# A transformer chain on one core: the last square of each norm goes straight into the summing products, and modulation columns move in their stage

## The chip, the cores and the metric

The kernel runs on 1 core of one Trainium2 chip. The metric is the device time of one execution in microseconds (us). TensorE does the matmuls, VectorE and ScalarE the element-wise work, GpSimd a few small operations, and SyncE (SP) issues the transfers from memory.

## What is computed

Two blocks run one after the other on 256 tokens of 1024 features, all in float32. Block one has two layers, each with a mixer (causal attention with forget gates, a short convolution and a pooling branch, merged by gates) and a feed-forward part. Block two has two layers as well, the first with a latent-attention mixer and the second with a dilated-attention mixer, each followed by a feed-forward part of 4096 features. Block two is modulated: six vectors per layer are computed from one vector `c` and scale, shift or gate the stream.

```python
cond = jax.nn.silu(c)
for i in range(2):
    mod = (cond @ ada_w[i] + ada_b[i]).reshape(B, 6, D)
    h = rms_norm(x, norm_mix[i]) * (1 + scale1) + shift1
    y = mla_mixer(h, ...) if i == 0 else dilated_mixer(h, ...)
    x = x + gate1 * y
    h = rms_norm(x, norm_mlp[i]) * (1 + scale2) + shift2
    x = x + gate2 * (jnp.square(jax.nn.relu(h @ mlp_w1[i])) @ mlp_w2[i])
```

with `rms_norm(x, g) = x * rsqrt(mean(x * x) + 1e-6) * g`, the mean taken over the 1024 features of a token.

## The kernel before

The stream `x` is held as eight tiles of 128 features by 256 tokens (features on the partitions). Weights come from memory in chunks of up to 1 MB into four raw buffers (`raw`). Each chunk is split into a high and a low part by `split_piece` (ScalarE casts `whi`, L319; VectorE subtracts `wlo`, L320), and every product is done as three matmuls of such parts in `mm3` (L368 to L374). `use` runs the transfers up to four chunks and the splits up to two chunks ahead.

**The norm.** The class `Norm` collects the sum of squares while the eight tiles of `x` are produced. For each tile m, ScalarE squares it (L441) and, from m = 1 on, GpSimd or VectorE adds it to the running sum (L446). `part1` sums the 128 partitions on TensorE by products with a matrix of ones (L452, one per half of the tokens; the hardware runs each as two instructions), VectorE scales and adds epsilon (L409), and GpSimd raises to the power -1/2 (L410). `part2` spreads the result over the partitions by products with the identity (L460). There are eight norms in all. Six of them are closed inside a projection that already runs on unnormalised inputs. The two at the start of the layers of block two are closed by `ada_h`, which has to have the result before it can form the inputs `h` (L1166 to L1170); `keep_warm` puts filler products (L1152) on TensorE around its steps.

**The modulation.** `ada_units(i)` is a generator: each step computes one of the 48 columns of `mod` of a layer, as a product and sum over 1024 elements on VectorE (L629). Every second step first issues the transfer of the next pair of columns (1 MB, L624) into one of the four raw buffers that the weights use too. Callers draw steps at fixed places of the loops. Steps of layer 1 carry a priority lowered by 3000.

**The stage around the change.** `mlp(i, h, tasks)` first runs 16 pairs of output tiles of the first matrix (loop over j = 0, 2, ..., 30; `fin` closes a tile), then eight output tiles of the second one (loop over m), each of which ends in `upd(m, a)`: the new `x[m]` (L1185), its square and its addition. With i = 0 it draws modulation steps. After it come `ada_finish(1, 0)`, the late `ada_h`, and the dilated attention of layer 1, where 24 further steps are drawn; `drain(ada1)` then runs whatever is left, just before the attention's output projection is finished and `mlp(1, h)` begins.

**What sets the order.** A planner orders each engine's instructions ahead of time by priority and by its own estimate of when things are ready; every engine then runs its queue strictly in that order. In the dilated attention stage and in the norm before it, TensorE's order is that of the program. `prio(m)` raises the updates of tiles 5 to 7.

Of the kernel before, what the change touches and what calls it, by code (L numbers as in the profile page):

```python
# [246 lines left out]
def tile_net(ctx, tc, wts, ada, xin, cols_in, table_in, fb_in, c_in, pos_in, inv_in, mask_in, freq_in, out):  # L247
# [22 lines left out]
    def bt(shape=(128, 512), dt=F32):  # L270
        return mk(big, list(shape), dt, "b")
# [4 lines left out]
    def t1(shape=(128, 256), dt=F32):  # L276
        return mk(t1p, list(shape), dt, "t1")
# [4 lines left out]
    def sm(n=1):  # L282
        return mk(smp, [128, n], F32, "sm")

    def acc():
        return mk(accp, [128, 512], F32, "acc")

    def att():
        return mk(attp, [128, 512], F32, "att")

    def cst(shape, dt, name):
        return const.tile(list(shape), dt, tag=name, name=name)

    V, S, G, PE = nc.vector, nc.scalar, nc.gpsimd, nc.tensor
# [67 lines left out]
    def mm3(o_ap, w, sl, x, start, stop, wmov=False, ns=324):  # L362


        whi, wlo = w[0][:, sl], w[1][:, sl]
        xhi, xlo = x
        if wmov:
            PE.matmul(out=o_ap, lhsT=xhi, rhs=whi, start=start, stop=False)  # L368
            PE.matmul(out=o_ap, lhsT=xhi, rhs=wlo, start=False, stop=False)  # L369
            PE.matmul(out=o_ap, lhsT=xlo, rhs=whi, start=False, stop=stop)  # L370
        else:
            PE.matmul(out=o_ap, lhsT=whi, rhs=xhi, start=start, stop=False)  # L372
            PE.matmul(out=o_ap, lhsT=whi, rhs=xlo, start=False, stop=False)  # L373
            PE.matmul(out=o_ap, lhsT=wlo, rhs=xhi, start=False, stop=stop)  # L374
        tick(ns)
# [9 lines left out]
    ones = cst([128, 128], F32, "ones")  # L385
# [20 lines left out]
    def rsqrt_small(r, ss, n, scale):  # L406

        v = sm(n)
        V.tensor_scalar(out=v[:, :n], in0=ss, scalar1=scale, scalar2=EPS, op0=ALU.mult, op1=ALU.add)  # L409
        G.tensor_tensor(out=r, in0=v[:, :n], in1=mhalf[:, :n], op=ALU.pow)  # L410
# [18 lines left out]
    class Norm:  # L429
# [9 lines left out]
        def add_(self, m, xt):  # L439
            q = t1()  # L440
            S.activation(out=q, in_=xt, func=AF.Square)  # L441
            if m == 0:
                self.s = q
            else:
                s = t1()
                (G if m < 6 and self.slow else V).tensor_tensor(out=s, in0=self.s, in1=q, op=ALU.add)  # L446
                self.s = s

        def part1(self):
            ps = att()  # L450
            for tt in range(2):
                PE.matmul(out=ps[:, 2 * tt:2 * tt + 2], lhsT=self.s[:, tt * 128:tt * 128 + 128],  # L452
                          rhs=ones[:, :2], start=True, stop=True)
            self.R = sm(2)
            rsqrt_small(self.R[:, :2], ps[:, 0:4:2], 2, 1.0 / D)

# [26 lines left out]
    def split_plain(dst, src):  # L483
        S.copy(out=dst[:, 0, :], in_=src)
        V.tensor_tensor(out=dst[:, 1, :], in0=src, in1=dst[:, 0, :].bitcast(F32), op=ALU.subtract)

    def parts(tl, sl=slice(None)):
        return tl[:, 0, sl], tl[:, 1, sl]
# [325 lines left out]
    def f1(bl, i0, xs, o_ap):  # L814
        for k, xt in enumerate(xs):
            w, sl = bl.at(i0 + k)
            mm3(o_ap, w, sl, xt, k == 0, k == len(xs) - 1)

    for l in range(2):
# [41 lines left out]
        for which in range(2):  # L861
# [8 lines left out]
            for tt in range(2):  # L870
                ps = a2[tt]
# [150 lines left out]
        bl, i = blk_state["bl"], blk_state["i"]  # L1022
# [49 lines left out]
        def upd(m, a):  # L1072
            with prio(m):
                upd_(m, a)
# [99 lines left out]
    def gated_update(i, s, nx, nrm, final=False, hs=None):  # L1174


        def upd(m, a):
            with prio(m):
                upd_(m, a)

        def upd_(m, a):
            xt = mk(xpool, [128, 256], F32, "x")
            gc = mod[:, 48 * i + 24 * s + 16 + m:48 * i + 24 * s + 17 + m]
            assert modc[0] >= 48 * i + 24 * s + 17 + m
            V.scalar_tensor_tensor(out=xt, in0=a[:, :256], scalar=gc, in1=x[m], op0=ALU.mult, op1=ALU.add)  # L1185
            nx.append(xt)
            if final:
                nc.sync.dma_start(out=out[m * 128:m * 128 + 128, :], in_=xt)
            else:
                if hs is not None:  # L1190
                    ht = mk(hpool, [128, 2, 264], F32R, "h")
                    o_ = 16 * i + 8 + m
                    split_scaled(ht[:, :, :256], xt, Gc[:, o_:o_ + 1])
                    sc = mod[:, 48 * i + 24 + m:48 * i + 25 + m]
                    S.copy(out=ht[:, 0, 256:258], in_=sc.to_broadcast([128, 2]))
                    V.tensor_tensor(out=ht[:, 1, 256:258], in0=sc.to_broadcast([128, 2]), in1=ht[:, 0, 256:258].bitcast(F32), op=ALU.subtract)
                    hs.append(ht)
                nrm.add(m, xt)
        return upd

    def mlp(i, h, tasks=None):
        bl = Blocks()
        hp_ = [parts(t, slice(0, 258)) for t in h]
        mid = []

        def fin(a):
            sh = sm(1)
            S.copy(out=sh, in_=a[:, 256:257])
            r = t1()
            V.tensor_tensor(out=r, in0=a[:, :256], in1=RB, op=ALU.mult)  # L1210
            S.activation(out=r, in_=r, func=AF.Relu, bias=sh)
            S.activation(out=r, in_=r, func=AF.Square)
            y = bt([128, 2, 256], F32R)
            split_plain(y, r)
            mid.append(y)

        held = []
        for j in range(0, 32, 2):
            a2 = [acc(), acc()]
            for k in range(8):  # L1220
                for e in range(2):
                    w, sl = bl.at((j + e) * 8 + k)
                    mm3(a2[e][:, :258], w, sl, hp_[k], k == 0, k == 7, ns=327)
                if j == 0 and k == 7:
                    nrm.part1()
                if j == 2 and k == 1:
                    nrm.part2()
                    RB, _ = nrm.rows(False)
                    fin(held[0])
                    fin(held[1])  # L1230
            if tasks is not None and j >= 4:
                next(tasks, None)
            if j == 0:
                held = a2
            else:
                for e in range(2):
                    fin(a2[e])
        mp = [parts(t) for t in mid]
        final = i == 1
        nrm2 = Norm()  # L1240
        nx = []
        upd = gated_update(i, 1, nx, nrm2, final)
        for m in range(8):
            a = acc()
            f1(bl, 256 + m * 32, mp, a[:, :256])
            upd(m, a)
            if tasks is not None:
                for _ in range(2):
                    next(tasks, None)
        bl.end(512)  # L1250
        return nx, nrm2
# [209 lines left out]
    out_proj8(bl, [parts(t) for t in oT], gated_update(0, 0, nx, nrm, hs=h), ahead_done[0])  # L1461
    x = nx
    x, nrm = mlp(0, h, chain(ada0, ada1))
    ada_finish(1, 0)

# [160 lines left out]
    out_proj8(bl, [parts(t) for t in oT], gated_update(1, 0, nx, nrm, hs=h), acs)  # L1626
    x = nx
    mlp(1, h)


# [33 lines left out]
```

## Time and profile before

| | |
|---|---|
| median of 3 runs | 1572.71 us (1570.24 to 1573.25) |
| the profiled execution | 1576.66 us, its span 1574.9 us |
| TensorE busy | 1550.7 us, 98% |
| VectorE busy | 1177.0 us, 75% |
| ScalarE busy | 899.6 us, 57% |
| GpSimd busy | 152.3 us, 10% |
| mean granted TensorE clock | 0.995 |
| moved from and to memory | 320.77 MB, mean 204 GB/s |

The span reaches from the first to the last instruction of one profiled execution; the execution's own time has a little more around it. Busy shares are means over all stages. Matmuls are pipelined, so the start-to-start distance of two matmuls is shorter than the duration that the trace gives to one.

### The profile page before, as it was taken

To read this page: it belongs to the slowest core of one execution; us is meant where nothing else is said; L and a number is where in the kernel's file an instruction comes from. 1 tells how busy PE (TensorE), PEld (TensorE's weight loads), DVE (VectorE), ACT (ScalarE), POOL (GpSimd) and SP (SyncE) were. 2 spreads that over 40 slices of the span, in tenths; PEclk is the share of its full clock that TensorE was granted. 3 is DMA by queue.
4 is the path that set the end of the run, shared out by engine and by line. 5 is a ranking of instruction groups with operands and counts; after the bars stand their busy time and mean duration, and the time that the engine had idled before them with its cause. 6 is when DMAs were issued, how large, how long until landed. Compare 5 with 4: busy or idle time off the path is not lost.

```text
span 1574.9 us, 31147 instructions
## 1 busy us (share of the span) xinstructions
PE 1550.7 (98%) x12314; PEld 1508.7 (96%) x12314; DVE 1177.0 (75%) x2430; ACT 899.6 (57%) x1854; POOL 152.3 (10%) x209
## 2 busy tenths in 40 slices
PE   9999999999999999999999999999999999999999
PEld 8899999999899999999987899999999999999999
DVE  7877877789787777778778688766777777686642
ACT  7575554443657454443268677533676766677632
POOL 2100100000210010000021100010223222110000
PEclk9999999999999999999999999999999999999999
DMA  8446566655655666665544278775666767655551
GB/s 308 174 173 218 208 241 216 235 183 170 209 193 190 232 227 226 214 240 179 170 133 138 81 244 284 272 270 201 218 213 213 221 199 241 195 203 186 191 198 41
DMA packets 83921, 320.77 MB, mean 204 GB/s; under 512 B 31984, under 2 KB 34800, under 8 KB 58944
## 3 DMA queue, kind: packets, MB, share of 16 engines
q1 hardware_dynamic: 83184, 317.30, 58.6%
q8 instruction: 97, 1.59, 0.4%
q0 software_dynamic: 448, 1.38, 0.3%
q14 instruction: 48, 0.39, 0.1%
q10 hardware_dynamic: 144, 0.11, 0.0%
HBM read 311.42 MB, written 7.34 MB: 202 GB/s over the span
## 4 chain that ended last, share of the span: by engine, by line
PE 91%; DVE 5%; issue 1%; ACT 1%; POOL 1%; DMA 1%; SPq 0%; ACTq 0%; DVEq 0%; POOLq 0%
PE acc L372 21%; PE acc L374 21%; PE acc L373 21%; PE acc L368 6%; PE acc L370 6%; PE acc L369 6%; DVE wlo L320 2%; PE att L767 1%; PE att L1546 1%; POOL sm L410 1%; PE att L1548 1%; PE att L1560 1%; PE att L680 1%; PE acc L713 1%; PE att L1577 1%
## 5 line engine op out<-in xcount | busy, mean ns | idle before, releaser
L320 DVE TENSOR_TENSOR wlo<-raw,whi 128x1024 fp32r<-128x1024 f32 (+2 forms) x508 | 582.3, 1165 | 150.7 <-ACT whi L319 149.8
L319 ACT CAST whi<-raw 128x1024 fp32r<-128x1024 f32 (+2 forms) x508 | 495.2, 1000 | 306.0 <-PE acc L373 183.3
L372 PE MATMUL acc<-b,whi 128*128 128x256 f32 x1744 | 496.4, 285 | 3.2 <-DVE sm L409 1.6
L373 PE MATMUL acc<-b,whi 128*128 128x256 f32 x1744 | 490.2, 281 | 0.0
L374 PE MATMUL acc<-b,wlo 128*128 128x256 f32 x1744 | 489.2, 281 | 0.0
L372 PE MATMUL acc<-h,whi 128*128 128x256 f32 (+1 forms) x1216 | 343.2, 282 | 0.0
L374 PE MATMUL acc<-h,wlo 128*128 128x256 f32 (+1 forms) x1216 | 342.4, 282 | 0.0
L373 PE MATMUL acc<-h,whi 128*128 128x256 f32 (+1 forms) x1216 | 341.5, 281 | 0.0
L372 PEld LDWEIGHTS acc<-b,whi 128*128 128x128 f32 x1744 | 328.3, 188 | 7.3 <-issue 4.0
L373 PEld LDWEIGHTS acc<-b,whi 128*128 128x128 f32 x1744 | 328.5, 188 | 1.2 <-issue 0.8
L374 PEld LDWEIGHTS acc<-b,wlo 128*128 128x128 f32 x1744 | 328.6, 188 | 0.1
L372 PEld LDWEIGHTS acc<-h,whi 128*128 128x128 f32 x1216 | 229.9, 189 | 0.0
L374 PEld LDWEIGHTS acc<-h,wlo 128*128 128x128 f32 x1216 | 229.2, 188 | 0.0
L373 PEld LDWEIGHTS acc<-h,whi 128*128 128x128 f32 x1216 | 229.1, 188 | 0.0
L368 PE MATMUL acc<-whi,h 128*128 128x384 f32 (+4 forms) x544 | 193.3, 356 | 1.9 <-ACT whi L319 1.9
L369 PE MATMUL acc<-wlo,h 128*128 128x384 f32 (+4 forms) x544 | 184.1, 339 | 0.4 <-DVE wlo L320 0.4
L370 PE MATMUL acc<-whi,h 128*128 128x384 f32 (+4 forms) x544 | 182.8, 338 | 0.0
L410 POOL TENSOR_TENSOR sm<-sm,mhalf 128x4 f32<-128x4 f32 (+3 forms) x72 | 93.0, 1292 | 508.8 <-DVE sm L409 468.9
L629 DVE CUSTOM_DVE_ANT_0 t<-raw,cond,cols 128x1024 bf16<-128x1024 f32 x96 | 121.7, 1278 | 11.3 <-DMA raw<-in_ada_dram 5.7
L368 PEld LDWEIGHTS acc<-whi,h 128*128 128x128 f32 x544 | 104.1, 192 | 6.1 <-ACT whi L319 2.1
L369 PEld LDWEIGHTS acc<-wlo,h 128*128 128x128 f32 x544 | 104.1, 191 | 3.4 <-DVE wlo L320 0.6
L370 PEld LDWEIGHTS acc<-whi,h 128*128 128x128 f32 x544 | 103.2, 190 | 2.8
(255 smaller groups left out, 1638.6 us busy)
## 6 DMA issues: line engine op xcount, KB each, us to landing
raw<-in_wts_dram SPq DMA_DIRECT2D x194, 1024.0 KB, 4.8
raw<-in_ada_dram SPq DMA_DIRECT2D x48, 1024.0 KB, 4.9
raw<-in_wts_dram SPq DMA_DIRECT2D x50, 768.0 KB, 4.5
scr<-b SPq DMA_DIRECT2D x48, 128.0 KB, 3.8
b<-scr SPq DMA_DIRECT2D x64, 96.0 KB, 5.3
raw<-in_wts_dram SPq DMA_DIRECT2D x6, 576.0 KB, 4.0
raw<-in_wts_dram SPq DMA_DIRECT2D x6, 512.0 KB, 3.5
raw<-in_wts_dram SPq DMA_DIRECT2D x3, 528.0 KB, 4.1
```

Source lines behind the costliest of these rows:

```text
L319: S.copy(out=hi[:, a:b], in_=r[:, a:b])
L320: V.tensor_tensor(out=lo[:, a:b], in0=r[:, a:b], in1=hi[:, a:b].bitcast(F32), op=ALU.subtract)
L368: PE.matmul(out=o_ap, lhsT=xhi, rhs=whi, start=start, stop=False)
L369: PE.matmul(out=o_ap, lhsT=xhi, rhs=wlo, start=False, stop=False)
L370: PE.matmul(out=o_ap, lhsT=xlo, rhs=whi, start=False, stop=stop)
L372: PE.matmul(out=o_ap, lhsT=whi, rhs=xhi, start=start, stop=False)
L373: PE.matmul(out=o_ap, lhsT=whi, rhs=xlo, start=False, stop=False)
L374: PE.matmul(out=o_ap, lhsT=wlo, rhs=xhi, start=False, stop=stop)
L410: G.tensor_tensor(out=r, in0=v[:, :n], in1=mhalf[:, :n], op=ALU.pow)
L629: V.tensor_tensor_reduce(out=junk, in0=w[:, e * 1024:e * 1024 + 1024], in1=cond, scale=1.0, scalar=col("ada_b", n), op0=ALU.mult, op1=ALU. ...
L680: PE.matmul(out=ps[:, 256 * i:256 * i + 256], lhsT=qk[:, 0, 128 * i:128 * i + 128], rhs=qk[:, 1, :], start=True, stop=True)
L713: PE.matmul(out=o_, lhsT=vcol(h0 + e, 0), rhs=pt[:, 0:256], start=True, stop=False)
```

## The change

In `Norm` the square of tile 7 is no longer added to the running sum. `part1` multiplies both the sum of the first seven squares and the last square with the matrix of ones and accumulates the two in the same place: four products instead of two. In `mlp` the modulation steps begin at j = 2 instead of j = 4, and none are drawn after output tiles 6 and 7. The stage so draws 15 + 12 = 27 steps instead of 14 + 16 = 30; three more are left for `drain(ada1)`, five instead of two.

```diff
             if m == 0:
                 self.s = q
+            elif m == 7:
+                self.last = q
             else:
...
-            for tt in range(2):
-                PE.matmul(out=ps[:, 2 * tt:2 * tt + 2], lhsT=self.s[:, tt * 128:tt * 128 + 128],
-                          rhs=ones[:, :2], start=True, stop=True)
+            for i, s in enumerate((self.s, self.last)):
+                for tt in range(2):
+                    PE.matmul(out=ps[:, 2 * tt:2 * tt + 2], lhsT=s[:, tt * 128:tt * 128 + 128],
+                              rhs=ones[:, :2], start=i == 0 and tt == 0, stop=i == 1 and tt == 1)
...
-            if tasks is not None and j >= 4:
+            if tasks is not None and j >= 2:
                 next(tasks, None)
...
-            if tasks is not None:
+            if tasks is not None and m < 6:
                 for _ in range(2):
                     next(tasks, None)
```

## Rows read from the trace of the kernel before

**Rows 1.** The page's busy table: engine, busy us, share of the span, instructions.
```profile
PE 1550.7 (98%) x12314; PEld 1508.7 (96%) x12314; DVE 1177.0 (75%) x2430; ACT 899.6 (57%) x1854; POOL 152.3 (10%) x209
```
**Rows 2.** TensorE's timeline, early norm: start, duration, instruction, [idle before <-releaser].
```profile
782.98 1.05 PE L1152 MATMUL att<-ones 128*128 128x128 f32 x8
786.38 0.58 PE L452 MATMUL att<-ones,t 128*128 128x2 f32 x4 [2.34 <-DVE t L446]
```
**Rows 3.** TensorE's timeline, late norm.
```profile
1087.35 1.73 PE L1152 MATMUL att<-ones 128*128 128x128 f32 x14
1091.24 0.61 PE L452 MATMUL att<-ones,t 128*128 128x2 f32 x4 [2.17 <-DVE t L446]
...
1093.18 1.23 PE L460 MATMUL att<-ident,sm 128*128 128x128 f32 x4 [0.78 <-POOL sm L410]
1094.19 2.77 PE L1152 MATMUL att<-ones 128*128 128x128 f32 x12
1096.62 0.67 PE L368 MATMUL acc<-whi,h 128*128 128x384 f32 x1
```
**Rows 4.** TensorE's timeline, the norm inside the projection at 910 us.
```profile
910.18 0.50 PE L452 MATMUL att<-ones,t 128*128 128x2 f32 x4
910.54 0.36 PE L372 MATMUL acc<-h,whi 128*128 128x258 f32 x1
```
**Rows 5.** VectorE's timeline (DVE), late norm.
```profile
1087.09 1.28 DVE L629 CUSTOM_DVE_ANT_0 t<-raw,cond,cols 128x1024 bf16<-128x1024 f32 x1 [2.60 <-DMA raw<-in_ada_dram]
...
1089.50 0.48 DVE L1185 SCALAR_TENSOR_TENSOR x<-acc,mod,x 128x256 f32<-128x256 f32 x1
```
**Rows 6.** ScalarE's timeline (ACT), late norm.
```profile
1087.47 0.83 ACT L319 CAST whi<-raw 128x768 fp32r<-128x768 f32 x1 [4.10 <-issue]
1090.08 0.42 ACT L441 ACTIVATE t<-x 128x256 f32<-128x256 f32 x1 [1.77 <-DVE x L1185]
```
**Rows 7.** The chain that ended last, before the late norm: start, duration, what.
```profile
1081.70 5.36 DMA raw<-in_ada_dram
```
**Rows 8.** ScalarE's timeline, early norm.
```profile
784.58 0.41 ACT L441 ACTIVATE t<-x 128x256 f32<-128x256 f32 x1
```
**Rows 9.** VectorE's timeline, early norm.
```profile
784.09 1.80 DVE L320 TENSOR_TENSOR wlo<-raw,whi 128x768 fp32r<-128x768 f32 x2
...
786.99 0.16 DVE L409 TENSOR_SCALAR sm<-att 128x2 f32<-128x2 f32 x1 [0.76 <-PE att L452]
```
**Rows 10.** One line's instructions, L446 and L452: count, duration min/median/max in ns, starts.
```profile
L446 DVE TENSOR_TENSOR t<-t,t x31: 407/419/426, 6.4 to 1392.0; 128x256 f32<-128x256 f32 x31
...
L452 PE MATMUL att<-ones,t x32: 167/251/330, 16.9 to 1394.5; 128*128 128x2 f32 x32
```
**Rows 11.** Stretches: us, busy of five engines, granted clock, DMA share, GB/s.
```profile
404.00:406.00 2.00, 1.34 (x11) 1.12 (x10) 1.54 (x3) 0.03 (x1) 1.50 (x1) 1.00 0.91 348
1094.00:1096.00 2.00, 2.00 (x11) 2.00 (x11) 1.56 (x4) 1.04 (x3) 0.00 (x0) 0.50 0.85 353
```
**Rows 12.** TensorE's timeline, the norms closed at 201 and 403 us.
```profile
205.03 0.71 PE L460 MATMUL att<-ident,sm 128*128 128x128 f32 x4 [0.55 <-POOL sm L410]
...
406.17 0.71 PE L460 MATMUL att<-ident,sm 128*128 128x128 f32 x4 [0.83 <-POOL sm L410]
```
**Rows 13.** The chain that ended last, behind the late norm.
```profile
1097.28 0.32 PE acc L369
...
1099.78 0.17 PE acc L369
```
**Rows 14.** VectorE's timeline, end of the dilated attention.
```profile
1375.61 0.42 DVE L485 TENSOR_TENSOR b<-att,b 128x256 fp32r<-128x256 f32 x1 [0.42 <-ACT b L484]
```
**Rows 15.** Stretches, the output projection after that attention.
```profile
1376.00:1395.00 19.00, 19.00 (x163) 18.92 (x162) 18.39 (x34) 14.90 (x32) 4.85 (x5) 1.00 0.59 194
```
**Rows 16.** GpSimd's timeline (POOL), the power in two norms.
```profile
404.50 1.62 POOL L410 TENSOR_TENSOR sm<-sm,mhalf 128x2 f32<-128x2 f32 x1 [80.62 <-DVE sm L409]
...
1092.42 0.71 POOL L410 TENSOR_TENSOR sm<-sm,mhalf 128x2 f32<-128x2 f32 x1 [15.10 <-PE att L1152]
```

## The prediction, made before the changed kernel ran

> **What bounds the kernel now.** I read the page's busy table first: TensorE is busy in 98% of the span [rows 1]. The kernel is a stream of matmuls; an edit on another engine counts only where TensorE stands still for it, while every product added to the stream counts in full. Next the list of TensorE's waits: the two longest on this code are at the summing products of two norms, L452, with 2.34 us at 786 us and 2.17 us at 1091 us, both for VectorE's last addition L446 [rows 2, 3]. These are the two norms that `ada_h` closes before any input of the next projection can be formed; I call them the early and the late one. The other six are closed inside running projections: at 910 us the products stand between projection matmuls with no gap [rows 4].
>
> The late norm is to be read engine by engine. The matmuls of output tile 7 end at about 1087.5, the filler products of `keep_warm` run from 1087.35 for 1.73 us, and then TensorE idles until 1091.24 [rows 3]. VectorE could have formed `x[7]` at once, but in its queue two modulation columns (L629) stand ahead: it first waits 2.60 us for their transfer, starts them at 1087.09, and `x[7]` starts only at 1089.50 [rows 5]. The square follows on ScalarE at 1090.08 [rows 6], then on VectorE a split piece and the addition. The chain that ended last goes through this very transfer [rows 7]. At the early norm no column stands in front: the square starts at 784.58 [rows 8], and VectorE is in two split pieces for 1.80 us from 784.09 before it can add [rows 9].
>
> **Columns no longer beside tiles 6 and 7.** Four columns leave the output loop and one (j = 2) joins the pair loop: 27 instead of 30 in the stage, 67 instead of 70 before the attention stage, where `ada_finish(1, 0)` needs 64. Without columns `x[7]` can start when its matmuls end, at 1087.5 instead of 1089.50: 2.0 us earlier. Its square comes behind a cast that holds ScalarE for 0.83 us from 1087.47 [rows 6], so it ends near 1088.7 instead of 1090.5.
>
> **Last square straight into the products.** One addition of 0.42 us per norm leaves VectorE [rows 10]. That is worth something only in the two exposed norms: there TensorE can sum the first seven squares ahead and waits for the last square alone.
> Late norm: TensorE comes out of the filler at 1089.08 (1087.35 + 1.73). The products of the old sum, four instructions, take 0.36 us by the norm at 910 us [rows 4], with the start after a gap some 0.4; so the last products start at 1089.5, when the square is long done, instead of 1091.24: **1.7 us**. Bounds: 0.8 if the power on GpSimd is slowed (below), 2.0 if all of the shift of `x[7]` comes through.
> Early norm: the old sum's products run in the idle time after the filler, which ends at 784.03 (782.98 + 1.05) [rows 2]; the last ones start behind the square at 785.05 (784.58 + 0.41 and a hand-over) instead of 786.38, 1.3 us earlier. But the scaling L409, now at 786.99, sits behind the split pieces that end at 785.89 [rows 9]. That leaves **1.1 us**. Bounds: 0.2, if the scheduler puts one more piece of 0.9 us (half of the two) in front of L409, and 1.3.
>
> **The clock.** After the late norm the granted clock is 0.50, the level of 1.2 GHz, in the window from 1094 to 1096 [rows 11]; before it TensorE had idled for 2.17 and 0.78 us [rows 3]. At 404 us it idled for 0.83 us alone and kept 1.00 [rows 11, 12]. After the change the late norm has some 0.9 us left, the wait for the power. What the low level costs: the first eight projection matmuls follow at 0.32 instead of 0.17 us [rows 13], 1.2 us; and the last twelve filler products take 2.43 us (1094.19 to 1096.62) where 14 took 1.73 [rows 3], 0.9 us, of which 0.6 counts, since the first `h` tile is then what is late next. I credit 1.0 of these 1.8, because the last `h` tiles, paced by VectorE, come due; bounds 0 and 1.8. For the early norm, whose idle time falls from 2.8 to about 1.3 us, I credit 0.3 of at most 0.9 us, half of the late norm's.
>
> **More products.** Each norm gets four more instructions at L452; now 32 serve eight norms [rows 10]. Four take 0.36 us up to the next matmul [rows 4], and that is paid in full at the norms of 586, 910 and 1394 us: 1.1 us. The first norm, at 17 us, runs on the lower clock; I take 0.4. At 201 and 403 us TensorE waits for the power afterwards anyway, 0.55 and 0.83 us [rows 12], behind a scaling that stands after a split piece: nothing is paid while that wait lasts, 0.36 us each without it. Together **1.5 us** lost; bounds 1.1 and 2.3.
>
> **Where the columns go.** The j = 2 column costs VectorE some 1.3 us near 910 us, hidden as long as the weight split runs a chunk ahead of TensorE; I take nothing, 1.3 us if that cover is gone. The 24 columns of the attention stage keep their places, their transfers move by one. At its end five columns are drained instead of two, and two transfers instead of one stand in front of the weights' on SP's queue. The pair drained now leaves VectorE a wait of 0.42 us before it splits the last attention output [rows 14]; behind that it is busy for 18.39 of 19 us [rows 15]. The three more columns (3.8 us) are gate columns of the last output loop and can wait until that stretch is over. I take nothing; bounds 0 and 4 us.
>
> **Sum.** -1.7 - 1.1 - 1.0 - 0.3 + 1.5 = -2.6 us. The profiled execution took 1576.66 us (span 1574.9 and 1.8 around it), 0.25% above the median 1572.71 of the runs shown. From its own time that gives 1574.1, from the median 1570.1.
>
> **Rivals.**
> *The gap shrinks, but little comes of it.* The power takes 0.71 us where VectorE is quiet and 1.62 us with a split piece right behind the scaling [rows 16]. As the late norm moves forward against the splits, a piece can fall just there: 0.9 us lost. If the clock falls all the same, 1.3 more. The edit may also miss its mark: columns are low-priority work that the scheduler fills in, and one whose data has landed may still stand in front of `x[7]`; then the late norm gives about the 0.7 us of addition and split piece. Each leaves between -0.3 and -1.7: about 1571.8.
> The Trainium skill, "SBUF — State Buffer", section "Who interferes with whom", says that a VectorE instruction with two SBUF inputs and a GpSimd instruction that reads SBUF shut each other out for their whole length, whoever starts first. The two durations of the power agree with it; by that rule the sum would be -1.7 with a piece there in one norm.
> *The clock stays up throughout.* 1.8 and 0.9 instead of 1.0 and 0.3: -4.0, or 1568.7. For it speaks the little idle time left; against it that the filler is thin work itself.
> *Slower: the drained columns.* If two of them are queued ahead of the updates of the attention's output projection, and their transfer is late by what the pair at 1087 waited, 2.60 us [rows 5], VectorE loses that and 2.5 us for the two, in a stretch where it has 0.6 us to spare [rows 15]. TensorE would lose some 4.5 us: net +1.9, 1574.6. The sign turns once that loss exceeds 2.6 us. Against it: low priority, and the one pair of now fits.
>
> **How the numbers follow.** Forecast 0.50 (own range 1568.5 to 1571.5), little comes of it 0.25, clock stays up 0.13, drained columns 0.12. A difference under 0.2%, 3.1 us, can hardly be told from none. The forecast's -2.6 crosses that line only with more of the clock's credit: a third of it and nearly all of the clock case make faster 0.29; slower takes most of the last case, 0.11; same is the rest, 0.60. The range, 1567.5 to 1575.0, reaches from the clock case with its bounds to the slow case.
>
> **What would show it.** Right: no L629 between tile 5's and the late norm's `x[7]`; `x[7]` within 0.1 us of the end of its matmuls; eight L452 instructions per norm, and the 31 additions on VectorE [rows 10] down to 23; the stall at the late L452 gone and the early one under 1 us; a shorter low stretch of the clock. Wrong: a column or a late transfer still in front of `x[7]`, new stalls between 1375 and 1400 us, or a power of 1.6 us in either exposed norm.

## The result, and the profile after

The changed kernel takes 1591.18 us (median of 4 runs, 1589.73 to 1592.19), the kernel before beside it 1572.98: a ratio of 1.0112, interval 1.0100 to 1.0123. It is **18 us slower**; the forecast was 1570.1, the range 1567.5 to 1575.0. The profiled executions show less of it. They took 1589.73 and 1576.66 us (spans of 1587.4 and 1574.9), the first 1.45 us below its median, the one of before 3.68 above: 13.07 + 1.45 + 3.68 = 18.20.

The page's busy table of the changed kernel, to be read against [rows 1]:

```profile
PE 1556.9 (98%) x12346; PEld 1513.4 (95%) x12346; DVE 1174.9 (74%) x2422; ACT 899.1 (57%) x1854; POOL 154.3 (10%) x209
```

The 32 further products and the 8 additions fewer on VectorE are there; TensorE is busy for 6.2 us more, the span is 12.5 longer. (Behind L452 the lines of the new kernel are numbered three higher; in the kernels with the old norm they are those of before.)

**The norms came out as forecast**, in the two traces. TensorE's timeline of the late norm, against [rows 3]:

```profile
1087.63 1.73 PE L1155 MATMUL att<-ones 128*128 128x128 f32 x14
1089.19 0.95 PE L455 MATMUL att<-ones,t 128*128 128x2 f32 x8
...
1091.82 0.71 PE L463 MATMUL att<-ident,sm 128*128 128x128 f32 x4 [1.13 <-POOL sm L410]
1092.37 1.50 PE L1155 MATMUL att<-ones 128*128 128x128 f32 x12
1093.65 0.44 PE L368 MATMUL acc<-whi,h 128*128 128x384 f32 x1
```

and VectorE's, against [rows 5]:

```profile
1087.83 0.48 DVE L1188 SCALAR_TENSOR_TENSOR x<-acc,mod,x 128x256 f32<-128x256 f32 x1 [3.06 <-PE acc L374]
...
1090.18 0.16 DVE L409 TENSOR_SCALAR sm<-att 128x2 f32<-128x2 f32 x1 [0.61 <-PE att L455]
1090.26 0.95 DVE L320 TENSOR_TENSOR wlo<-raw,whi 128x768 fp32r<-128x768 f32 x1
```

`x[7]` waits for its matmuls and nothing else, the eight products run without a stall, and from the filler's start to the first projection matmul it is 6.02 us (1087.63 to 1093.65) where it was 9.27. At the early norm the last products wait 0.67 us for the square instead of 2.34 for the addition, and TensorE is at the next step 1.1 us sooner:

```profile
785.20 0.61 PE L455 MATMUL att<-ones,t 128*128 128x2 f32 x4 [0.67 <-ACT t L441]
```

Behind the late norm the granted clock is now 1.00 throughout (1092 to 1102 us), where it was 0.50 from 1094 to 1098. Behind the early norm it still falls to 0.50 (788 to 790 us; before, 790 to 792).

**Where the time went.** GpSimd's power L410 runs 76 times in each kernel and makes good marks. The table gives its start, minus that in the profiled execution of before, at eight of them, and the same difference of the spans. (The first column holds what differs up to 587 us, most of it by chance: it is subtracted where stretches are compared. With the new norm 0.36 to 0.37 us of it are no chance: they arise between the marks at 439 and 587 us, in every kernel that has it and in no other, around the norm closed at 586 us.)

| kernel | 587.46 | 787.24 | 910.96 | 1109.00 | 1127.22 | 1137.91 | 1360.04 | 1395.24 | span |
|---|---|---|---|---|---|---|---|---|---|
| changed | +0.08 | -1.01 | -0.52 | -5.63 | -4.60 | +1.72 | +2.02 | +11.65 | +12.5 |
| changed, second profile | +0.46 | -0.65 | -0.15 | -5.26 | -4.23 | +2.10 | +3.13 | +12.33 | +13.3 |
| before, second profile | -0.49 | -0.50 | -0.49 | -3.37 | -3.36 | -3.49 | -3.38 | -3.39 | -3.4 |
| norm alone | +0.79 | -0.30 | +0.20 | -3.05 | -3.10 | -2.84 | -3.04 | -2.76 | -1.8 |
| 28 steps | +1.88 | +0.79 | +1.26 | -2.01 | -2.06 | -1.70 | -1.99 | +0.09 | +2.5 |
| pairs recut | +1.41 | +0.31 | +0.78 | -2.47 | -2.52 | -2.54 | -2.46 | -0.38 | +0.9 |
| pair closed at the end | +0.93 | -0.17 | +0.37 | -4.74 | -3.70 | +2.63 | +3.38 | +9.04 | +11.5 |
| bias loads on GpSimd | -0.83 | -1.93 | -1.50 | -6.62 | -5.46 | -4.34 | -4.60 | -1.01 | +1.7 |
| columns alone | -1.46 | -1.47 | -1.87 | -7.87 | -6.82 | -0.50 | +0.54 | +5.96 | +6.9 |
| odd alone | +0.74 | +0.73 | +0.76 | -3.97 | -2.93 | +3.40 | +4.36 | +9.49 | +10.4 |
| 30 steps | +0.70 | -0.39 | -1.26 | -4.53 | -4.57 | -4.61 | -4.51 | -4.22 | -3.3 |

By 1109 us the changed kernel is 5.7 us ahead, of which it gives 1.0 back by 1127. Then it loses 6.3 us in one place, between 1127 and 1138 us, and 9.6 us in another, between 1360 and 1395 us. The first loss and most of the second lie in the dilated attention of layer 1, a stage that the diff doesn't touch. What the diff does touch there is the parity of its columns: two steps share one transfer and one raw buffer, and an odd number, 27, was drawn before the stage.

*The first loss.* SyncE's queue in the changed kernel (a row is a run of transfers of one kind; b is the bias of the attention scores, read back from `scr` in eight loads for each group of heads):

```profile
1106.66 10.61 SPq L310 DMA_DIRECT2D raw<-in_wts_dram  x4
1117.37 5.80 SPq L1539 DMA_DIRECT2D b<-scr  x8
1123.26 0.56 SPq L627 DMA_DIRECT2D raw<-in_ada_dram  x1
1125.84 8.55 SPq L310 DMA_DIRECT2D raw<-in_wts_dram  x3
```

and in the kernel before:

```profile
1120.80 4.48 SPq L310 DMA_DIRECT2D raw<-in_wts_dram  x3
1125.37 8.26 SPq L1536 DMA_DIRECT2D b<-scr  x8
1133.73 0.56 SPq L310 DMA_DIRECT2D raw<-in_wts_dram  x1
1134.38 0.38 SPq L624 DMA_DIRECT2D raw<-in_ada_dram  x1
```

Before, three weight chunks were under way ahead of the bias; now the columns' transfer takes a buffer first and the weights start at 1125.84. VectorE, then TensorE, show what that does:

```profile
1132.21 1.83 DVE L320 TENSOR_TENSOR wlo<-raw,whi 128x768 fp32r<-128x768 f32 x2 [4.66 <-ACT whi L319]
1133.96 1.28 DVE L632 CUSTOM_DVE_ANT_0 t<-raw,cond,cols 128x1024 bf16<-128x1024 f32 x1
...
1135.16 0.55 DVE L1553 CUSTOM_DVE_ANT_0 t<-att,b 128x384 f32<-128x384 f32 x1
```

```profile
1137.85 0.52 PE L1563 MATMUL att<-ident,t 128*128 128x128 f32 x3 [4.00 <-DVE sm L1555]
```

The split of the late weights, and a column behind it, stand in VectorE's queue ahead of the scores (L1553); TensorE, in program order, stands still for 4.00 us. Behind this wait the granted clock falls too (columns as in [rows 11]):

```profile
1140.00:1142.00 2.00, 2.00 (x8) 1.81 (x8) 0.97 (x4) 0.00 (x0) 1.39 (x2) 0.50 0.00 0
```

It is 1.00 again from 1144 us. The next products of L1563 start 5.97 us after these (1143.82); in the kernel before the distance is 4.36 us (1137.50 to 1141.86). TensorE is busy all the time between them, so the clock costs another 1.6 us.

*The second loss.* Here the roles are turned. The pair issued at 1347.46 is split: its second column is drawn only by `drain` (L632 at 1379.12), and it holds one of the four buffers until then. Each weight transfer now waits for a buffer, and the bias loads of the last group wait behind it. The chain that ended last:

```profile
1359.35 5.04 DMA b<-scr
...
1364.41 1.39 DVE wlo L320 x2
1365.81 0.02 issue
1365.83 0.33 SPq L310
1366.16 0.05 issue
1366.21 7.35 DMA b<-scr
```

The split pieces end at 1365.80 and free a buffer, the weight transfer is issued at 1365.83, and only then the last five bias loads, from 1366.21. In the kernel before seven of the eight are issued in one run:

```profile
1355.91 5.20 SPq L1536 DMA_DIRECT2D b<-scr  x7
```

In the changed kernel VectorE and TensorE wait for them:

```profile
1373.72 0.56 DVE L1553 CUSTOM_DVE_ANT_0 t<-att,b 128x384 f32<-128x384 f32 x1 [5.00 <-DMA b<-scr]
```

```profile
1376.07 0.52 PE L1563 MATMUL att<-ident,t 128*128 128x128 f32 x3 [3.00 <-DVE t L657]
1378.21 0.87 PE L1563 MATMUL att<-ident,t 128*128 128x128 f32 x3 [0.92 <-DVE t L657]
```

Then the clock goes, as the stretches show (columns as in [rows 11]):

```profile
1370.00:1378.00 8.00, 4.29 (x34) 3.86 (x33) 2.45 (x11) 2.00 (x8) 0.00 (x0) 0.98 0.33 65
1378.00:1386.00 8.00, 6.32 (x45) 5.28 (x46) 2.90 (x9) 2.32 (x9) 0.00 (x0) 0.50 0.40 132
```

TensorE was busy for 4.29 of 8 us, and for the 8 us after that the granted clock is 0.50, the level of 1.2 GHz.

*A wait behind both.* It is not the pair's. At the last norm the drained columns stand on both sides of the scaling L409 in VectorE's queue, the power comes late, and TensorE waits for it:

```profile
1405.45 1.28 DVE L632 CUSTOM_DVE_ANT_0 t<-raw,cond,cols 128x1024 bf16<-128x1024 f32 x1
...
1406.65 0.15 DVE L409 TENSOR_SCALAR sm<-att 128x2 f32<-128x2 f32 x1
1406.73 1.27 DVE L632 CUSTOM_DVE_ANT_0 t<-raw,cond,cols 128x1024 bf16<-128x1024 f32 x1
```

```profile
1408.62 0.71 PE L463 MATMUL att<-ident,sm 128*128 128x128 f32 x4 [1.63 <-POOL sm L410]
```

In the kernel before TensorE doesn't wait there; with the norm alone it waits 0.50 us, with 28 steps 2.20 and with the pairs recut 2.25. Both have no pair across a border, so it is the number of drained columns that counts here, and it makes up most of the 2.1 us that they lose between the last two marks.

### The profile page after: what moved, and what is told of

Same layout as the page of the kernel before. It is cut to its first block, busy times and chain, and to the rows that moved or that the text cites. A ratio compares the mean times of both kernels' runs of the same rounds, so it can differ in the third digit from the quotient of the medians.

```text
span 1587.4 us, 31205 instructions
## 1 busy us (share of the span) xinstructions
PE 1556.9 (98%) x12346; PEld 1513.4 (95%) x12346; DVE 1174.9 (74%) x2422; ACT 899.1 (57%) x1854; POOL 154.3 (10%) x209
## 4 chain that ended last, share of the span: by engine, by line
PE 89%; DVE 5%; issue 2%; ACT 2%; POOL 1%; DMA 1%; POOLq 0%; SPq 0%; DVEq 0%; ACTq 0%
PE acc L372 21%; PE acc L374 21%; PE acc L373 21%; PE acc L368 6%; PE acc L370 6%; PE acc L369 6%; DVE wlo L320 2%; POOL sm L410 1%; PE att L770 1%; DMA b<-scr 1%; PE att L1549 1%; PE att L1563 1%; PE att L1551 1%; PE att L683 1%; PE acc L716 1%
## 5 line engine op out<-in xcount | busy, mean ns | idle before, releaser
L410 POOL TENSOR_TENSOR sm<-sm,mhalf 128x4 f32<-128x4 f32 (+3 forms) x72 | 95.2, 1323 | 511.8 <-DVE sm L409 478.3
L632 DVE CUSTOM_DVE_ANT_0 t<-raw,cond,cols 128x1024 bf16<-128x1024 f32 x96 | 122.1, 1279 | 7.2 <-PE att L699 3.4
```

Source lines behind the costliest of these rows:

```text
L632: V.tensor_tensor_reduce(out=junk, in0=w[:, e * 1024:e * 1024 + 1024], in1=cond, scale=1.0, scalar=col("ada_b", n), op0=ALU.mult, op1=ALU. ...
```

## The experiments

My theory: it is the pair that lies across the border between two stages. It shifts the transfers of the whole attention stage by one step and leaves a buffer occupied at the end, and SyncE's queue, in which weights and bias loads stand in one line, turns both into stalls. Two rivals: the three more columns drained beside the last norm; and the new norm, which moves the planner's order everywhere behind it.

**The norm alone** (columns as in the kernel before).

```diff
-            if tasks is not None and j >= 2:
+            if tasks is not None and j >= 4:
...
-            if tasks is not None and m < 6:
+            if tasks is not None:
```

> The norm part alone, columns as before. Theory (an odd number of modulation steps in the stage splits a pair of columns, so that one raw buffer stays occupied and the weight and bias transfers behind it on SP's queue come late): the norm part is innocent, 1570 to 1573 us (early norm -1.0, late norm about -0.7, more products +1.0), no stall between 1120 and 1140 or 1365 and 1385 us. Rival 1 (more columns and transfers to drain at the end of the attention): the same. Rival 2 (the norm edit moves the planner's order and so the stalls): 1585 us or more.

1574.19 us, ratio 1.0005 (0.9993 to 1.0016), a little above the expected range. The norm loses nothing that the times show, and gains nothing either: a question for later.

**The columns alone** (the kernel before, with the columns of the changed one).

> The column part alone, norm as before: 27 steps, five columns drained. Theory and rival 1: both stalls are there, 1589 to 1593 us. Rival 2: about 1571 us.

1584.99 us, ratio 1.0071 (1.0054 to 1.0088). Both losses are there: TensorE waits 4.0 us for VectorE in the first, and the last power starts 5.4 us later, counted from the one at 1360 us. But that is 5.4 and not 9.6 us, and the time is 4 us short of the expected range: the old norm has a smaller second loss (see the last experiment).

**One more step**: 28 drawn, four drained, still two transfers in the drain.

```diff
-                for _ in range(2):
+                for _ in range(3 if m == 5 else 2):
```

> The changed kernel with a third step after output tile 5: 28 steps, an even number, four columns and two transfers drained. Theory: no pair is split at the start or the end of the attention stage, both stalls go, the gain at the norms stays: 1567 to 1571 us. Rival 1: four instead of five columns and still two transfers, 1584 to 1591 us.

1576.81 us, ratio 1.0018 (1.0008 to 1.0028). One step more takes away 14 of the 18 us; the time is far from the rival's range, but 6 us above that of the theory. The first loss is gone (-2.06, then -1.70 in the table). Between the last two marks 2.1 us are left, most of them the delay of the last power by the drained columns.

**Odd alone**: the kernel before with one step fewer, at the front (29 drawn, three drained in one transfer, columns beside all tiles, old norm).

```diff
-            if tasks is not None and j >= 4:
+            if tasks is not None and j >= 6:
```

> The kernel before with steps from j = 6 on instead of j = 4: 29 steps, an odd number; columns still beside tiles 6 and 7, three columns and one transfer drained. Theory: the split pair alone brings both stalls, 1582 to 1590 us. Rival 1: one column more and no transfer more than before, 1573 to 1577 us.

1585.23 us, ratio 1.0072 (1.0056 to 1.0088). A single step taken from the kernel before costs 11 us, with one more column drained and no more transfer for it: what costs is that the number of steps is odd.

**The pair closed at the end**: the changed kernel, one more step in the last attention group.

```diff
-            if n_ in (2, 10, 19):
+            if n_ in (2, 10, 19) or (hp == 7 and n_ == 22):
```

> The changed kernel with one more column step, drawn in the last attention group (27 + 25 steps, 4 columns drained), so that the second column of the last pair leaves its buffer before the attention ends. The first loss of the changed kernel (6.3 us between the GpSimd powers at 1127 and 1138 us) is not touched. Theory (a transfer brings two columns; an odd number of steps in the MLP stage leaves a pair half used at the stage's end and moves every later transfer by one step): the first loss stays at 6 to 6.5 us, the second (9.6 us between the powers at 1360 and 1395 us) shrinks to 1 to 6 us, because the buffer comes free but the bias loads still stand behind weight transfers on SP: 1582 to 1588 us beside 1574 of the kernel before. Rival (what costs is the columns drained beside the last norm): one column fewer there, two transfers still: 1590 us, with both losses as they were.

1587.58 us, ratio 1.0086 (1.0067 to 1.0106). The first loss is untouched (6.3 us), the second 5.7 instead of 9.6: both as the theory has it.

**The bias loads on GpSimd's queue**, otherwise the changed kernel.

```diff
-                nc.sync.dma_start(out=b_[64 * e:64 * e + 64], in_=src.rearrange("(s q) k -> q s k", q=64))
+                nc.gpsimd.dma_start(out=b_[64 * e:64 * e + 64], in_=src.rearrange("(s q) k -> q s k", q=64))
```

> The changed kernel with the 64 bias loads of the attention groups issued by GpSimd instead of SP. Theory (the stalls come because bias loads and weight transfers stand in one line on SP, behind a transfer that waits for one of the four buffers): the waits for the bias loads near 1374 us go, the second loss falls from 9.6 to 2 to 5 us, and the first, where weights stand behind the waiting transfer, at least shrinks: 1578 to 1586 us. Rival (SP's order is not what counts, but that a buffer is held): both losses stay, 1589 to 1593 us. If GpSimd's own instructions wait behind these loads, its powers and split pieces come late all through the attention, and the time is above 1593 us.

1578.77 us, ratio 1.0034 (1.0022 to 1.0045). The split pair is still there and holds its buffer, but 12 us are gone: the first loss shrinks from 6.3 to 1.1 us, the second from 9.6 to 3.6. TensorE has no wait left near 1130 us, and its longest at the end is 2.26 us at the last norm, as with the pairs recut. So the held buffer alone does little in this kernel; what made it dear is that one queue carries both.

**The pairs recut**: 27 steps and five drained columns as in the changed kernel, but the column at each border comes in a transfer of its own.

```diff
-        for n0 in range(0, 48, 2):
+        cut = [*range(0, 48, 2), 48] if i == 0 else [*range(0, 20, 2), *range(19, 48, 2), 48]
+        for n0, n1 in zip(cut, cut[1:]):
```

> The changed kernel, its 27 steps and its 5 drained columns unchanged, but the pairs cut anew: the 19th column of the second half (the last one of the MLP stage) comes in a transfer of its own, and so does the last, so that no pair lies across a border of stages; one more transfer in all. Theory (it is the pair across the border, not the number of steps or of drained columns): SP's order in the attention stage is that of the kernel before, both losses go, and what the three drained transfers cost at the last norm stays: 1575 to 1579 us. Rival (five drained columns cost it): 1588 to 1592 us.

1577.20 us, ratio 1.0021 (1.0010 to 1.0032). The steps, and the columns beside the last norm, are those of the changed kernel; 14 us are gone. One stretch of this kernel and the same of the changed one, where TensorE idles for 4.00 of 16 us:

```profile
1124.00:1140.00 16.00, 16.00 (x101) 15.69 (x100) 11.23 (x30) 9.32 (x24) 4.98 (x8) 1.00 0.84 244
```

```profile
1124.00:1140.00 16.00, 12.00 (x71) 11.52 (x70) 9.50 (x22) 7.17 (x18) 1.28 (x4) 0.96 0.64 220
```

**Thirty steps**, none beside the last two tiles, two drained.

```diff
-                for _ in range(2):
+                for _ in range(3 if m < 3 else 2):
```

> The changed kernel with three column steps instead of two beside the first three output tiles: 15 + 15 = 30 steps in the MLP stage as before, 2 columns drained in one transfer as before, none beside the last two tiles. Theory: the transfers of the attention stage stand where they stood before, both losses go entirely, and what is left is the gain at the two norms that the traces of the changed kernel showed (1.0 at the first, 1 to 2 more by the last, up to 5.6 by the first attention group at 1109 us, of which the kernel of before's columns with the new norm already has 3): 1570 to 1573 us beside 1574 of the kernel before. Rival (something else of the columns' new places costs, so that only the old places are good): 1576 us or more.

1574.74 us, ratio 1.0004 (0.9992 to 1.0015). Neither loss is left in the trace, and its span is 3.3 us under that of before. Yet the median is the same and misses the expected range. The same columns with the old norm, run next, complete the four combinations.

> The kernel before with the columns of the 30-step placement (from output pair 2 on, three beside the first three output tiles, two beside the next three, none beside the last two) and its old norm. With it the four combinations of old and new norm and old and good columns are complete. By the sum of the prediction: without the new norm the early gap stays as it is (its 2.3 us idle time), the late one loses the columns in front of the last tile (1.5 to 2.5 us) if those cost anything in most executions: 1571 to 1573 us beside 1574; if they cost only in the profiled execution of before: 1574, no change.

1574.82 us, ratio 1.0004 (0.9993 to 1.0014): same, as expected if the columns in front of `x[7]` cost only in the execution that I had read. And with 32 steps and no column left to drain (`range(2 if m == 5 else 3)`):

> The changed kernel with three steps beside each of the first five output tiles and two beside the sixth: 32 steps in the MLP stage, 24 in the attention, no column left to drain beside the last norm, none beside the last two tiles. Theory (a pair across a border and columns drained at the end are what costs): both losses of the changed kernel are gone and the end gains what the two drained columns of the kernel before cost beside its last norm, 0.5 to 2 us: 1570 to 1573.5 us. Rival (the denser columns in the MLP stage keep VectorE and SP's line from the split pieces there): 1575 us or more.

1574.62 us, ratio 1.0002 (0.9991 to 1.0012): same, a little above the range expected by the theory and just under the rival's 1575.

**The kernel before once more**, for a second profile: it asks where the norm's gain of the first traces has gone.

> The kernel before once more, unchanged, for a second profile of it. In the traces so far everything that the new norm saves adds up to about 2.6 us between the GpSimd powers at 587 us and the end (first norm 1.1 saved, the norm at 911 us 0.5 lost, last norm 1.4 saved by its power and 1.8 more by the first attention group, the end 0.9 lost), yet the kernel with the new norm alone has the same median as before. Theory A (the profiled execution of before was a slow one at its last norm: the column transfer in front of the last residual tile was issued at 1081.70 us there and at 1080.0 to 1080.2 in the two experiments that keep it, which save their 1.7 by that alone): the second profile shows the transfer near 1080, an idle time of 0.6 us instead of 2.17 before the summing products, and the power about 1.5 us earlier. Theory B (the late transfer belongs to the kernel): 2.2 us again, and the medians hide a real gain in the spread of the runs' starts.

Theory A. The median is 1573.93 us (ratio 1.0005, 0.9993 to 1.0018), but at the late norm of the second profile SyncE issues the transfer early, and TensorE hardly waits:

```profile
1078.73 0.38 SPq L624 DMA_DIRECT2D raw<-in_ada_dram  x1
```

```profile
1086.85 1.73 PE L1152 MATMUL att<-ones 128*128 128x128 f32 x14
1089.19 0.61 PE L452 MATMUL att<-ones,t 128*128 128x2 f32 x4 [0.61 <-DVE t L446]
...
1094.21 0.62 PE L368 MATMUL acc<-whi,h 128*128 128x384 f32 x1
```

0.61 us instead of 2.17, and 7.36 us from the filler to the projection instead of 9.27. From the mark at 587 to that at 1109 this execution is 2.9 us shorter than the one that I had read.

**VectorE made to wait for the power**: with new norm and no column drained, a small copy of the power's result on VectorE right behind it.

```diff
             rsqrt_small(self.R[:, :2], ps[:, 0:4:2], 2, 1.0 / D)
+            V.tensor_copy(out=sm(2)[:, :2], in_=self.R[:, :2])
```

> The kernel with no column drained and the new norm (32 steps in the MLP stage), and one small copy of the norm's two columns on VectorE behind the power, so that VectorE's next instruction waits for GpSimd's power instead of running beside it. In all traces with the new norm a split piece stands directly behind the scaling, and the power takes 1.72 us at 911 us, 1.28 to 1.29 at 1092 us and 1.62 to 1.72 at the last norm, where it takes 0.71 in the kernel before. In VectorE's order the copy stands directly behind the scaling at all norms but two; at those two (near 586 and 1092 us) one split piece is still between them. Theory (VectorE's work beside the power slows it): 0.71 us at 404, 911 and at the last norm, still about 1.3 at 1092, TensorE's waits for the power at 911 and at the last norm (0.50 each) gone: 1.0 us shorter there, up to 1 us more at 404 us: 1572.5 to 1574 us beside 1574.6 of the same kernel without the copy. Rival (the new norm's power is slow for its own reason, or the late split pieces cost what the power saves): durations or time as without the copy, 1574 to 1576 us.

The power in the norm at 910 us, with the norm alone and with the copy, and the stretch around it in the same order:

```profile
911.16 1.72 POOL L410 TENSOR_TENSOR sm<-sm,mhalf 128x2 f32<-128x2 f32 x1 [7.70 <-DVE sm L409]
```

```profile
909.87 0.71 POOL L410 TENSOR_TENSOR sm<-sm,mhalf 128x2 f32<-128x2 f32 x1 [7.73 <-DVE sm L409]
```

```profile
905.00:916.00 11.00, 10.50 (x88) 10.29 (x87) 7.58 (x13) 6.73 (x15) 1.72 (x1) 1.00 0.68 224
```

```profile
905.00:916.00 11.00, 11.00 (x95) 11.00 (x95) 8.52 (x13) 6.69 (x16) 0.71 (x1) 1.00 0.71 244
```

Theory right: 0.71 us there and at the last norm, 1.29 at the late one, and TensorE no longer idles. At 404 us it stayed at 1.62, since a split piece stands between there too, which I had misplaced. 1572.87 us, ratio 0.9999 (0.9990 to 1.0009): the half microseconds are real in the trace and too small for the times. No version here beats the kernel before by what can be measured.

**The changed kernel once more.**

> The changed kernel once more, unchanged, for a second profile. Its median lies 7 us above those of the two kernels with an odd number of steps and the old norm (1585.0 and 1585.2 us), and in its first profile the second loss is 9.6 us where theirs are 5.1 to 5.4: the bias loads there leave VectorE idle for 5.00 us in one piece where theirs leave 2.8 to 3.1, TensorE 3.00 where theirs leave 0.8 to 1.1, and the granted clock falls to 0.50 for some 8 us. Theory A (the long wait belongs to this kernel, by its later weight transfers): 4.5 to 5 us on VectorE, about 3 on TensorE and the clock at 0.50 again, second loss 9 to 11 us. Theory B (that execution's bias loads happened to be slow): 2.8 to 3.2 us on VectorE, a second loss of 5 to 6 us, and the remaining 2 to 5 us of the median lie elsewhere.

Theory A: 1590.58 us, ratio 1.0094 (1.0064 to 1.0123), and again a long wait and the low clock:

```profile
1374.40 0.56 DVE L1553 CUSTOM_DVE_ANT_0 t<-att,b 128x384 f32<-128x384 f32 x1 [4.57 <-DMA b<-scr]
```

```profile
1380.00:1384.00 4.00, 3.01 (x27) 2.45 (x25) 1.59 (x4) 1.12 (x6) 0.00 (x0) 0.50 0.37 124
```

So the second loss of 9.2 to 9.6 us, against 5.1 to 5.4 with the old norm, belongs to this kernel: its longer wait keeps TensorE's clock down for longer, as the last section shows. Why the five bias loads take longer here (4.00 and 3.83 us to issue, 3.27 in the two kernels with the old norm) stays open.

## Why the prediction was wrong

**The step that failed** is "Where the columns go", and in it the sentence "The 24 columns of the attention stage keep their places, their transfers move by one", with "I take nothing; bounds 0 and 4 us". The fact was right and the price wrong: the move costs 6.3 us at 1130 us and, with the pair that stays open at the stage's end, most of the 9.6 at 1375 us. I had priced the steps where they are computed, at 1.3 us of VectorE each, and the transfers only where the drain issues two instead of one. I followed none of the other transfers to what stands behind it on SyncE's queue, although all weights and bias loads of eight attention groups stand there. Recutting the pairs (14 us back at equal steps) and odd alone (11 us for one step) show the cause; the other queue for the bias loads (12 us back) shows the way that it takes.

**The rival "Slower: the drained columns"** had the right sign and a small part of the cause. With the parity mended and four or five columns drained in two or three transfers, the kernels take 1576.8 and 1577.2 us; with two or none 1574.6 to 1574.7. That is 2 to 3 us, against the 4.5 that I gave it, and in another place: not at the updates of the output projection but at the norm behind it, where TensorE waits 1.63 us in the changed kernel and 2.20 and 2.25 in these two. "New stalls between 1375 and 1400 us", named as a sign of error, came, but for the bias, not for the drained columns; the first loss, at 1130 us, I had not looked for at all.

**The early norm**, -1.1: right to a tenth. In all kernels with the new norm the mark at 787 us moves by 1.09 to 1.11 us against that at 587. The further -0.3 for its clock did not come: the clock still falls there, and in the changed kernel the next power, at 800 us, is no further ahead than the one at 787. In the profiles of 30 steps, of none drained and of the copy the clock stays at 1.00 there, and the power at 800 us is a further 1.3 us ahead; their medians show nothing of it.

**The late norm**, -1.7, and **the clock**, -1.0: right against the execution that I read, where the low stretch of the clock is gone, and wrong as a gain. From 911 to 1109 us the changed kernel gains 5.1 us and the norm alone 3.3; but the kernel before gains 2.9 by itself in its second profile, because the transfer in front of `x[7]` is issued 2.5 us earlier (1078.73 against 1081.70, less the 0.5 by which that execution is ahead there). Against it the norm alone gains 0.4 us. The changed kernel's lead at 1127 us, 4.1 us counted from 911, is no gain of columns taken away from `x[7]` either: odd alone, which keeps them and the old norm, has 3.7. The working took a chance delay of one profile, 2.60 us on one transfer, for a property of the kernel. The median, 3.7 us under the profiled execution, was the warning; I had used it only to shift the sum.

**More products**, +1.5: the size is about right (its upper bound adds up to 2.2, not 2.3), and part of it has another cause. Eight products instead of four take 0.95 us where they took 0.50 [rows 4]. At the norm of 586 us they cost 0.36 to 0.37 us in every kernel that has them, as the working had it. From 787 to 911 us the norm alone loses 0.5 us, from 1360 to 1395 us 0.3, and behind the last mark 1.0. Nearly all of the last is the power, which I had under "The gap shrinks, but little comes of it": the columns alone and odd alone have the old products and a last power of 1.68 us and lose 0.9 us behind that mark, and the kernel with the copy has the new products and a power of 0.71 us and loses 0.2. With the new norm, the kernel with the copy apart, another VectorE instruction starts directly behind the scaling at the norms of 911, 1092 and 1395 us (a split piece; at the last one in the changed kernel a column), and the power takes 1.72, 1.28 to 1.29 and 1.62 to 1.72 us there; in both profiles of the kernel before it takes 0.71 at all three. The order on VectorE does this and not the norm by itself, since three kernels with the old norm have a slow power at one of these norms too (1.61 to 1.68 us). With the norm alone it leaves TensorE idle for 0.50 us at each of two norms, little beside 18.
The Trainium skill, "SBUF — State Buffer", section "Who interferes with whom", has VectorE with two inputs and a reading GpSimd shut each other out for the whole instruction. The runs agree: at 911 us the piece that starts just ahead of the power lasts 1.2 us, the power takes 1.0 longer, and with VectorE held back by the copy it takes 0.71. In the kernel before the piece starts 0.38 us behind the power (911.34 against 910.96), and the power takes 0.71 as well.

**Sum of the norm.** Early -1.1, products and powers +0.5, +0.3 and +1.0, late -0.4: counted from the mark at 587 us the norm alone ends 0.3 us behind the second profile of the kernel before, and with the products at 586 us 0.7, which its ratio of 1.0005 allows. The 2.6 us of the forecast were not there to be had in most executions, apart from what the columns lost.

**What stays open.** Which part of the first loss is due to the late weights and which to the column that stands behind their split (1.28 us) was not separated. A fifth raw buffer would have tried the buffer by itself; it wasn't tried.

## What to carry to other kernels

When a generator issues a transfer on every second step, an odd number of steps moved across a stage's border moves every later transfer: write down the order of the in-order queue in the stages that the diff doesn't touch as well, and ask at each shared buffer who frees it and what stands behind the transfer that needs it. Keep the number even, or cut the pairs at the border. And where the profiled execution lies well above the median, profile the kernel a second time before crediting the removal of a long wait in it.

## What the runs showed of the hardware

Late transfers cost TensorE twice, once in idle time and once in clock. At the first loss, behind 4.00 us of idle time, the granted clock was 0.50 from 1140 to 1142 us and 1.00 from 1144. At the second, with idle times of 1.06, 0.92 and 1.19 us among the last scores (the columns alone) the mean granted clock was 0.93 from 1376 to 1380 us, 0.64 in the next four and 1.00 after that; with 3.00, 0.92 and 0.53 us (the changed kernel) it was 0.50 for the whole 8 us from 1378. And a power of two columns on GpSimd, 0.71 us by itself, took up to 1.72 us beside one split piece on VectorE.
